# A two-layer hybrid decoder step: three plain fp32 products rewritten as sums of rounded high and low parts

## The chip, the cores and the metric

The kernel runs on one core of a Trainium2 chip. The metric is the time of one execution in microseconds (us); a smaller number is better. Each time given for a kernel is the median of several executions, and one further execution is profiled instruction by instruction.

## The reference

One inference step goes through two layers. A prompt of 512 tokens and eight single sample tokens are handled together, so that T = 520 columns run through the shared weights. Three places of the layer matter here.

- **Page compression.** The compressed branch of the sparse attention cuts the cached key and value rows into blocks of 32 tokens at a stride of 16 and passes each through a small two-layer network: `gelu(flat @ w1) @ w2`, where `flat` has 32 x 64 numbers per block. Keys and values have weights of their own. There are 32 cached pages of 128 rows, four for each of the eight samples, and the prompt's own rows are compressed in the same way.
- **Channel mean.** The convolution branch normalizes its 256 channels: `mu = mean(x)`, `xc = x - mu`, and so on.
- **Pointwise product.** After that normalization and a swish follows `y @ w_pw + b_pw` with a 256 x 256 matrix.

## The kernel before, in words

The kernel keeps channels on the 128 partitions and tokens along the columns. Each big projection (24 tiles of `w_in`, 8 tiles of `w_out` per layer) is made by `product` (L744): both operands were split beforehand into a high part, rounded to the type float32r (`F32R`), and a low part, the rest, and three products high x high, high x low and low x high are added in PSUM. A split (`split`, L724) is two instructions: a copy that rounds, and a subtraction that gives the rest. One tile of a projection takes 8 chunks x 3 products x 2 halves of 260 columns (`HALF`, L362) = 48 matmuls.

Three products still run on plain fp32 operands:

- `compress` (L878) is called four times in a layer, for keys and values (`kv`) and for two groups of pages (`hb`). It multiplies eight 128 x 128 chunks of `w1` (loaded in `cmp_weights`, L867) by the pages, ten at a time: 160 moving columns, or 112 for the last seven pages of the first group. That is 16 matmuls for a call, 64 for a layer.
- `conv_norm` (L1070) makes the channel mean with the constant matrix `mean_w` (L1078, four matmuls of 260 columns for a layer).
- `conv_norm` makes the pointwise product with `raw`, the weights `w_pw` (L1100, eight matmuls of 260 columns for a layer).

Nothing is issued where it stands in the code. The functions only record operations (`Plan.add`, L236), grouped into units; a unit is one operation, or several of the tensor engine under `plan.burst()`. `Plan.place` (L286) then puts the units into the sequence of a long list of numbers, `order` (L395), and gives each buffer the first fitting place when its turn comes. Within an engine the instructions run in that sequence; engines wait for one another by semaphores. Where an elementwise operation may run on one of several engines (`ch(...)`), the letter string `engines` (L386) says which: v is VectorE, s ScalarE, g GpSimd. All loads and stores go out on SyncE's queue; a page of the cache needs its number read from the page table first (`paged`, L611, with the register load at L616). All recorded operations are issued from one line, L352, so that the profile shows that line for nearly everything, and instructions are told apart by engine, operation and shape.

Buffers live in regions (L383): the region `d` has five places of 2,560 columns, and each page tile `pg` takes one of them, as do `x4`, `yo`, `zc` and `yoh`.

Of the kernel before, what the change touches and what calls it, by code (L numbers as in the profile page):

```python
# [9 lines left out]
F32R = mybir.dt.float32r  # L10
# [179 lines left out]
class Plan:  # L190
# [135 lines left out]
    def emit(self, tc, ctx):  # L326
# [60 lines left out]
        "vvvvgvvsssssvssgsvvggvggsvsvvssvvsgvvssvsvggsvvvgvgssgsggvvvgvsgsgsgvvggvvvsvvvvvssvsvsvsgggsvvvsvsgvgvsvgvgvssv"  # L387
        "vvsgsgsvssgvvsggsvgvsgsvsvggsvsggsvvggvggggvvssgvsssvsvsvggvvsgsgvggvvgvvgsssssggggssssvssssssvgvvggvvsvsvsgsgvv"
        "vsvvsvgsvvgvggssvvssvsvvvsvgvggggsgsvvgggggsvgvgvsssgvssvsssssvssssvsssgggvvvggsvgvvvvgvgsssssvvssvvsvvsgvvggsgg"
        "ggvggvvgvgsvvvvgsgsvvvsvgvsvsgvgsgsvsvsvsvggsvsgssggssvsvvvgvvgvgvggsvvsssvsvsssvssvgvvsssggggggvgvvvgsgsvvgssvg"  # L390
        "vsvgvsvvgsvssggvvsvgvvgvvggvsvvvvsvgvgvssvggsvvvsvssvgvsgvggvgsvggsgsgsgvgggvsggggvvvssgsvsvvsvsvsgggsgggvggvggs"
        "gsggssggssssvgsssvsvssvsgggsgvvsggvggvggvsggvssvsgvsgggssssvssvsvvvsssgvvggvggsgvvsssgggvgvgvsssssssssvsvvsvvsss"
        "sgvgvgvgvgvgvvvggvssvvvvssgvsvsvvsggvsgggvvsgsggvvsgsvgvsgggsggvsgggsgsgsvsvsvsvggvv"
    ),
    "order": (  # L395
# [146 lines left out]
def step_kernel(ctx: ExitStack, tc: tile.TileContext, i, o, tune=None):  # L542
# [82 lines left out]
    def constants():  # L625
        ve.memset(ones, 1.0)
        sc.activation(junk, ones[:, :1], AF.Exp)
        ve.memset(mean_w, 1.0 / 256.0)
        warm = plan.bank("warm", "t")
        for n in range(WARM // 2):  # L630
            with plan.burst():
# [85 lines left out]
    def layer(l):  # L717
        z_ = Layer()
# [824 lines left out]
```

## Time and profile before

| | us |
|---|---|
| median of 3 runs | 624.89 |
| lowest and highest run | 624.7, 625.42 |
| profiled execution, its own time | 623.73 |
| profiled execution, span from first to last instruction | 622.0 |
| TensorE matmul (PE) busy | 606.4 |
| TensorE weight load (PEld) busy | 536.7 |
| VectorE (DVE) busy | 433.7 |
| ScalarE (ACT) busy | 259.7 |
| GpSimd (POOL) busy | 226.2 |

A matmul's record lasts longer than the time until the next one can start, since matmuls are pipelined. The time that a matmul takes from its neighbours is therefore read as the distance from start to start (the pitch), and a row of a stretch of equal matmuls gives it as (length of the stretch - length of one record) / (count - 1). A plain fp32 matmul shows as two records, a matmul on float32r operands as one.

### The profile page before, as it was taken

To read this page: it belongs to the slowest core of one execution; us is meant where nothing else is said; L and a number is where in the kernel's file an instruction comes from. 1 tells how busy PE (TensorE), PEld (TensorE's weight loads), DVE (VectorE), ACT (ScalarE), POOL (GpSimd) and SP (SyncE) were. 2 spreads that over 40 slices of the span, in tenths; PEclk is the share of its full clock that TensorE was granted. 3 is DMA by queue.
4 is the path that set the end of the run, shared out by engine and by line. 5 is a ranking of instruction groups with operands and counts; after the bars stand their busy time and mean duration, and the time that the engine had idled before them with its cause. 6 is when DMAs were issued, how large, how long until landed. Compare 5 with 4: busy or idle time off the path is not lost.

```text
span 622.0 us, 15002 instructions
## 1 busy us (share of the span) xinstructions
PE 606.4 (97%) x5526; PEld 536.7 (86%) x5526; DVE 433.7 (70%) x1222; ACT 259.7 (42%) x731; POOL 226.2 (36%) x250
## 2 busy tenths in 40 slices
PE   6999999999999999999999999999999999999997
PEld 5999998898868788579999999999985968677997
DVE  6535879966778697965465498887677678688221
ACT  4102125656683395431221132237575769543100
POOL 2123225442414363341522242556443535144700
PEclk9999999999999999999999999999999999999999
DMA  8755444322652346887546234342246135788622
GB/s 267 217 166 180 152 124 146 115 76 73 136 122 65 104 125 220 268 252 228 185 143 194 85 113 160 94 124 62 77 79 155 37 95 140 185 255 252 208 77 95
DMA packets 89130, 90.98 MB, mean 146 GB/s; under 512 B 25858, under 2 KB 59746, under 8 KB 88930
## 3 DMA queue, kind: packets, MB, share of 16 engines
q1 hardware_dynamic: 89058, 90.04, 48.9%
q8 instruction: 43, 0.70, 0.5%
q14 instruction: 29, 0.24, 0.1%
HBM read 75.32 MB, written 14.67 MB: 145 GB/s over the span
## 4 chain that ended last, share of the span: by engine, by line
PE 84%; DVE 6%; SPq 5%; DMA 3%; issue 2%; ACT 1%; ACTq 0%; DVEq 0%
PE banks L352 84%; DVE t L352 4%; SPq L352 3%; DVE small L352 2%; DMA t<-in_win 2%; SPq L616 1%; ACT t L352 1%; DMA t<-in_x 1%; DMA t<-in_cmp 0%; DVE keep L352 0%; ACTq L352 0%; DVEq L352 0%
## 5 line engine op out<-in xcount | busy, mean ns | idle before, releaser
L352 PE MATMUL banks<-t,t 128*128 128x260 f32 (+5 forms) x3960 | 490.0, 302 | 1.9 <-DVE t L352 0.8
L352 PEld LDWEIGHTS banks<-t,t 128*128 128x128 f32 (+3 forms) x3960 | 434.2, 178 | 32.8 <-issue 25.1
L352 POOL TENSOR_TENSOR t<-t,t 128x512 fp32r<-128x512 f32 (+4 forms) x84 | 111.4, 1332 | 129.2 <-PE banks L352 55.7
L352 ACT ACTIVATE t<-t 128x512 fp32r<-128x512 f32 (+4 forms) x130 | 78.5, 613 | 155.1 <-DVE t L352 56.8
L352 ACT ACTIVATE t<-t,small 128x384 f32<-128x384 f32 (+4 forms) x185 | 99.2, 552 | 16.2 <-DVE small L352 15.9
L352 PE MATMUL banks<-keep,t 128*128 128x128 f32 (+7 forms) x698 | 87.2, 311 | 1.9 <-DVE t L352 1.1
L352 DVE TENSOR_TENSOR t<-t,t 128x512 fp32r<-128x512 f32 (+3 forms) x92 | 71.0, 782 | 22.0 <-PE banks L352 16.0
L352 PEld LDWEIGHTS banks<-keep,t 128*128 128x128 f32 (+2 forms) x698 | 66.5, 161 | 22.1 <-issue 12.5
L352 DVE TENSOR_TENSOR t<-banks,t 128x520 f32<-128x520 f32 (+1 forms) x54 | 37.2, 693 | 63.8 <-PE banks L352 51.2
L352 DVE CUSTOM_DVE_ANT_0 t<-banks,keep,small 128x384 f32<-128x384 f32 (+3 forms) x128 | 64.3, 528 | 16.2 <-PE banks L352 16.0
L352 POOL TENSOR_SCALAR t<-t 128x512 fp32r<-128x512 f32 (+2 forms) x49 | 34.6, 707 | 88.3 <-PE banks L352 48.5
L352 ACT ACTIVATE t<-banks 128x512 f32<-128x512 f32 (+3 forms) x72 | 36.6, 525 | 62.1 <-PE banks L352 45.7
L352 PE MATMUL banks<-t,keep 128*32 128x130 f32 (+7 forms) x688 | 41.2, 306 | 6.7 <-DVE keep L352 4.8
L352 PEld LDWEIGHTS banks<-t,keep 128*32 128x32 f32 (+3 forms) x688 | 23.2, 116 | 20.5 <-DVE keep L352 5.0
L352 POOL TENSOR_SCALAR t<-t,small 128x384 f32<-128x384 f32 (+3 forms) x50 | 32.9, 671 | 21.2 <-DVE small L352 15.4
L352 ACT ACTIVATE small<-small 128x32 f32<-128x32 f32 (+3 forms) x76 | 23.5, 310 | 27.5 <-DVE small L352 27.4
L352 DVE COPY t<-banks 128x512 f32<-128x512 f32 (+2 forms) x37 | 21.5, 589 | 11.2 <-PE banks L352 7.3
L352 DVE SCALAR_TENSOR_TENSOR t<-t,t 128x520 f32<-128x520 f32 (+2 forms) x32 | 27.8, 873 | 1.3 <-ACT t L352 1.1
L352 POOL TENSOR_TENSOR t<-t,keep 128x520 f32<-128x520 f32 (+1 forms) x11 | 14.2, 1296 | 33.5 <-DVE t L352 20.4
L352 POOL TENSOR_TENSOR t<-t 128x520 f32<-128x520 f32 (+1 forms) x12 | 12.8, 1068 | 33.2 <-DVE t L352 13.9
L352 ACT ACTIVATION_READ_ACCUMULATOR t<-t,small 128x1 f32 x132 | 24.7, 187 | 0.0
L352 DVE SCALAR_TENSOR_TENSOR small<-small 128x130 f32<-128x130 f32 (+3 forms) x80 | 23.5, 296 | 1.5
(81 smaller groups left out, 358.1 us busy)
## 6 DMA issues: line engine op xcount, KB each, us to landing
t<-in_w_in SPq DMA_DIRECT2D x96, 256.0 KB
t<-in_cmp SPq DMA_DIRECT2D x64, 128.0 KB
t<-in_slc SPq DMA_DIRECT2D x64, 128.0 KB
t<-in_w_out SPq DMA_DIRECT2D x32, 256.0 KB
t<-in_x SPq DMA_DIRECT2D x16, 260.0 KB
t<-in_win SPq DMA_DIRECT2D x16, 256.0 KB
out_win<-t SPq DMA_DIRECT2D x16, 256.0 KB
t<-glu SPq DMA_DIRECT2D x12, 264.0 KB
```

What stands on the lines that cost most here:

```text
L352: fn(*[real(v) for v in o.a], **{k: real(v) for k, v in o.k.items()})
L616: pages[n] = tc.nc.sync.value_load(pt.real(plan)[0:1, n:n + 1], min_val=0, max_val=n_phys - 1)
```

## The change

The weights `w1` are split once a layer, into two more buffers each (`cmp_weights`). In `compress` each half of a page group is split into a high and a low part, both in one new buffer of the kind `pg`, and each plain matmul becomes three on float32r parts, in one burst. In `conv_norm` the input of the mean is split and multiplied, high and low, by a rounded copy of the constant matrix (1/256 is exact in it): two matmuls for one. The pointwise weights and its input are split, and three matmuls take the place of one. The string `engines` has 816 letters where it had 756 (60 more choices, 30 splits of two), and both lists are new from end to end.

```diff
+    mean_r = new("c", [128, 128], F32R, fixed=True)
...
         ve.memset(mean_w, 1.0 / 256.0)
+        ve.tensor_copy(mean_r, mean_w)
...
         def cmp_weights():
...
-                z_.w1.append(w)
+                parts = [new("w1", [128, 8, 128], F32R) for u in "hl"]
+                split(w, *parts, "gv")
+                z_.w1.append(parts)
...
         def compress(kv, pg, first):
...
-            w, nb = z_.w1[kv], 17 if first else 20
+            (wh, wl), nb = z_.w1[kv], 17 if first else 20
...
             for h, (a, b) in enumerate(((0, 10), (10, nb))):
-                xs = pg[h][:, :b - a].rearrange("p b (k c g q) -> p k c g b q", k=2, c=8, g=2)[:, kv]
+                src = pg[h][:, :b - a, 128 * kv:128 * kv + 128]
+                parts = new("pg", [128, 2, 10, 128], F32R)
+                parts = [parts[:, u, :b - a] for u in range(2)]
+                split(src, *parts)
+                xh, xl = (v.rearrange("p b (c g q) -> p c g b q", c=8, g=2) for v in parts)
                 for cc in range(8):
-                    te.matmul(po[:, :, a:b], w[:, cc, :], xs[:, cc], start=(h == cc == 0), stop=(cc == 7),
-                              skip_group_check=True)
+                    with plan.burst():
+                        for n, (w, x_) in enumerate(((wh, xh), (wh, xl), (wl, xh))):
+                            te.matmul(po[:, :, a:b], w[:, cc, :], x_[:, cc], start=(h == cc == n == 0),
+                                      stop=(cc == 7 and n == 2), skip_group_check=True)
...
         def conv_norm():
...
+            wh, wl = (new("wpw", [128, 2, 256], F32R) for u in "hl")
+            split(raw, wh, wl, "gv")
...
             for c in range(2):
+                parts = [P("cy", F32R) for u in "hl"]
+                split(yv[c], *parts)
                 with plan.burst():
-                    for k, (a, b) in enumerate(HALF):
-                        te.matmul(pm[:, k], mean_w, yv[c][:, a:b], start=(c == 0), stop=(c == 1))
+                    for n, v in enumerate(parts):
+                        for k, (a, b) in enumerate(HALF):
+                            te.matmul(pm[:, k], mean_r, v[:, a:b], start=(c == n == 0), stop=(c == n == 1))
...
+                parts = [P("cy", F32R) for u in "hl"]
+                split(yv[c], *parts)
+                z_.cy.append(parts)
...
-                for c in range(2):
+                for c, (yh, yl) in enumerate(z_.cy):
                     with plan.burst():
-                        for k, (a, b) in enumerate(HALF):
-                            te.matmul(pm[:, k], raw[:, c, 128 * m:128 * m + 128], yv[c][:, a:b], start=(c == 0), stop=(c == 1))
+                        for n, (w, v) in enumerate(((wh, yh), (wh, yl), (wl, yh))):
+                            for k, (a, b) in enumerate(HALF):
+                                te.matmul(pm[:, k], w[:, c, 128 * m:128 * m + 128], v[:, a:b],
+                                          start=(c == n == 0), stop=(c == 1 and n == 2))
```

## Rows read from the trace of the kernel before

**Rows 1.** The page's head and part 1: busy time, share, instructions.

```profile
span 622.0 us, 15002 instructions
...
PE 606.4 (97%) x5526; PEld 536.7 (86%) x5526; DVE 433.7 (70%) x1222; ACT 259.7 (42%) x731; POOL 226.2 (36%) x250
```

**Rows 2.** The page's part 4: the chain that ended last, by engine.

```profile
PE 84%; DVE 6%; SPq 5%; DMA 3%; issue 2%; ACT 1%; ACTq 0%; DVEq 0%
```

**Rows 3.** Waits of PE: in total us, times, longest us.

```profile
PE banks L352 <- DVE keep L352: 4.8, 1, 4.8
PE banks L352 <- DVE t L352: 2.8, 5, 0.9
PE banks L352 <- POOL t L352: 1.0, 1, 1.0
PE banks L352 <- DMA t<-in_win: 0.8, 2, 0.7
PE banks L352 <- DMA t<-in_cmp_w: 0.6, 1, 0.6
PE banks L352 <- ACT t L352: 0.6, 1, 0.6
PE banks L352 <- DMA t<-in_cmp: 0.5, 1, 0.5
PE banks L352 <- DVE small L352: 0.4, 1, 0.4
```

**Rows 4.** Stretches: length, busy us (instructions) of PE, PEld, DVE, ACT, POOL; PEclk, DMA, GB/s.

```profile
12.00:62.00 50.00, 47.85 (x415) 46.15 (x416) 25.16 (x62) 10.53 (x20) 12.80 (x11) 1.00 0.63 191
311.00:370.00 59.00, 59.00 (x555) 56.52 (x554) 37.79 (x89) 11.23 (x21) 16.59 (x15) 1.00 0.44 138
```

**Rows 5.** Groups of PE by form, whole span: busy us, mean ns of a record.

```profile
L352 PE MATMUL banks<-t,t 128*128 128x260 f32 x3104 | 413.6, 289 | 0.8 <-DVE t L352 0.8
...
L352 PE MATMUL banks<-t,t 128*128 128x160 f32 x192 | 36.2, 303 | 1.1 <-DMA t<-in_cmp_w 0.6 <-DMA t<-in_cmp 0.5
...
L352 PE MATMUL banks<-t,t 128*128 128x112 f32 x64 | 10.3, 271 | 0.0
...
L352 PE MATMUL banks<-t,keep 128*128 128x260 f32 x16 | 3.9, 389 | 0.0
```

**Rows 6.** PE in order of time, four stretches: start us, length us, first form, count.

```profile
57.50 2.06 PE L352 MATMUL banks<-t,t 128*128 128x160 f32 x14
...
197.95 1.92 PE L352 MATMUL banks<-t,keep 128*128 128x260 f32 x8
...
230.60 0.82 PE L352 MATMUL banks<-t,t 128*128 128x260 f32 x3
...
280.76 13.97 PE L352 MATMUL banks<-t,t 128*128 128x260 f32 x115
```

**Rows 7.** Narrow plain matmuls: a group in 48.9 to 49.35, two timeline rows.

```profile
L352 PE MATMUL banks<-t,t 128*128 128x112 f32 x4 | 0.6, 271 | 0.0
...
250.62 0.36 PE L352 MATMUL banks<-small,keep 128*128 128x6 f32 x2 [0.40 <-DVE small L352]
250.84 0.37 PE L352 MATMUL banks<-t,t 128*128 128x260 f32 x1
```

**Rows 8.** Instructions of today's splits, by form, one row for each engine and operation.

```profile
L352 DVE CAST t<-t 128x512 fp32r<-128x512 f32 x27 | 12.4, 464 | 4.0 <-DMA t<-in_w_in 3.6 <-PE banks L352 0.3
...
L352 DVE TENSOR_TENSOR t<-t,t 128x512 fp32r<-128x512 f32 x76 | 60.6, 804 | 21.8 <-PE banks L352 16.0 <-POOL t L352 3.1 <-issue 1.2
...
L352 ACT ACTIVATE t<-t 128x512 fp32r<-128x512 f32 x72 | 44.9, 627 | 80.6 <-DMA t<-in_w_in 22.0 <-DMA t<-in_w_out 17.4 <-POOL t L352 12.8
...
L352 POOL TENSOR_TENSOR t<-t,t 128x512 fp32r<-128x512 f32 x68 | 91.9, 1355 | 116.0 <-PE banks L352 55.3 <-ACT t L352 33.2 <-DVE t L352 16.5
```

**Rows 9.** Chain of waits between 21 and 50 us, shares.

```profile
by line: SPq L352 44.4%; SPq L616 27.3%; issue 20.9%; DMA t<-in_cmp 7.7%
```

More of the change, by code (lines that the diff above doesn't have):

```diff
@@ L386 @@
     "engines": (
[L387 to L393, printed above, removed]
+        "gssvssgssvvsssvsggvvsgvvvvgvsvsvsvsvsgvvvvvvsssvsssssssvsvsvvvvsssssgsggvvgvgvvvsvgvsvsgvvvsgvvsvsgsvvggvvssvvvv"
+        "sgvvsgssggvsvvgsvssvvvsgsvvvssvvgsggsvgvsvvggvggsgsgsgvgsgvvvsvggsggssssvsgvggggvsvggsgsgvsssvsvgsvvsvvsgsvvvsss"
+        "vsvvgsgvgvvvgvggvggvvsvvsssvvsvsvsvssssvvssvsssggvvsgggggggsvssgvgvgvgssgsgvssgggssvssvssvssssvsssssssvggvvsggvg"
+        "vggggvgssssvsvgsvvssssgsgsgvvggggsvgvvvvsvggsgsvvgggsgsgggvvvvsvvvsvgvgvvsgggvgsvvssvsgsvgvvvvvvggvvgvvgsvsvssvs"
+        "gsvvvvvssggssvsvvvggvggvvssvgvsgsvvvsvgvsvsvvvsvvggsvvvgvvvsvsggsvgsvvvgsvvgsvvvgvvsvgggvssvvgsgsgsvsgvgvgggsvsv"
+        "vvsgsvvvsgsggvssvsvsgssgvgsssvsvsvgvgsgsvsgggvggvvssggsvsgvggssssvssvssvvvvggsgvgsgggggvsvggsggggsvsvvvvgvvssvss"
+        "sssvsvvggvvsgvgsvggvggsgvvggsggvssvsgggssggvsgsssvsvsvsssssvsggsvvvgvsgvgvvggsssvssvvgsvvsvssggvgsgsgsgggsgggvgv"
+        "vvsvsggvsggvgvgvgggvgvgvsgvvsggv"
     ),
     "order": (
[140 rows of a table removed]
[143 rows of a table added]
     ),
@@ L1071, in conv_norm @@
             yv = z_.conv
+            z_.cy = []
             raw = new("wpw", [128, 2, 256])
             ld(raw, i["w_pw"][l])
+            wh, wl = (new("wpw", [128, 2, 256], F32R) for u in "hl")
+            split(raw, wh, wl, "gv")
             pm = plan.bank("pm", "mm", 2)[:, :, :T // 2]
             for c in range(2):
+                parts = [P("cy", F32R) for u in "hl"]
+                split(yv[c], *parts)
                 with plan.burst():
-                    for k, (a, b) in enumerate(HALF):
-                        te.matmul(pm[:, k], mean_w, yv[c][:, a:b], start=(c == 0), stop=(c == 1))
+                    for n, v in enumerate(parts):
+                        for k, (a, b) in enumerate(HALF):
+                            te.matmul(pm[:, k], mean_r, v[:, a:b], start=(c == n == 0), stop=(c == n == 1))
             sq = []
```

283 rows, old and new, of the table TUNE are left out of this document.

## The prediction

> **What bounds the kernel now.** I read the busy times first. The tensor engine has a record open for 606.4 of 622.0 us, every other engine has 188 us or more to spare [rows 1]. The chain that ended last agrees: 84% of it is PE [rows 2]. Then I asked who keeps PE waiting: the eight waits sum to 11.5 us, of which 4.8 us is the single wait at the very start [rows 3]. So some 7 us of the whole run is PE standing still for somebody, and whatever adds work to PE adds it to the end. The reader should see that elsewhere a microsecond is nearly free, and on PE it costs a microsecond. The two stretches that hold the page compression, one in each layer, say the same: PE is busy for 47.85 of 50 us in the first and for all 59 us of the second, while VectorE, ScalarE and GpSimd are free for half the time or more in the first, and VectorE for a third in the second [rows 4].
>
> So the change must be costed in PE's pitch, start to start. Four stretches give it. A record of the plain compression at 160 columns: (2.06 - 0.303) / 13 = 0.135 us [rows 5, 6], two records, so **0.270 us** a matmul. A plain record at 260 columns: (1.92 - 0.389) / 7 = 0.219 us for the mean, (0.82 - 0.389) / 2 = 0.22 for the pointwise product [rows 5, 6], **0.438 us** a matmul. A float32r matmul at 260 columns in the projections: (13.97 - 0.289) / 114 = **0.120 us** [rows 5, 6].
>
> Two of these show something else. If a plain record sweeps its columns twice, one sweep of 260 costs 0.219 / 2 = 0.110 us, and the float32r matmul at 0.120 is slower than its one sweep: the columns are not what paces it. And narrow plain records do not get cheaper in proportion: at 160 columns 0.135, at 112 columns (0.6 - 0.271) / 3 = 0.11 rather than the 0.095 of the proportion, and at 6 columns still (250.84 - 250.62) / 2 = 0.11 [rows 7]. Each record has a weight load of its own, 5526 for 5526 [rows 1]. I read this as a floor: a load of 128 fp32 weight columns paces the engine at 0.110 to 0.120 us, however few columns follow.
>
> **The change, part by part.**
>
> *Compression.* Today 192 records x 0.135 + 64 x 0.11 = 25.9 + 7.0 = 32.9 us. After it, 128 matmuls become 384, each one record. None has more than 160 columns, so each is under the floor. No row shows a float32r matmul with fewer than 260 columns and 128 weight columns, so I bound it: from below by the plain floor of 0.110 (384 x 0.110 = 42.2 us), from above by the wider float32r matmul, 0.120 (46.1 us). Same operand type as the upper, fewer columns: I take 0.116, 44.5 us. That is **+11.6 us** (+9.3 to +13.2). The change triples the number of weight loads and saves only sweeps, and at this width the sweeps were the smaller part.
>
> The Trainium skill's page "TensorE: Matmul & The Clock Gate" says under "Back-to-back issue gap" that a warm matmul costs N / 2.4 + 2.5 ns, which is 69 and 49 ns at 160 and 112 columns and 111 at 260; by that alone compression would cost 24.6 us, mean and pointwise 1.7 us less each, and the run would take about 613 us. The same page under "LDWEIGHTS" puts a load at columns / 1.2, 107 ns for 128, which is the floor; the rows with 6 columns side with this one.
>
> *Mean.* 16 records x 0.219 = 3.5 us become 16 matmuls x 0.120 = 1.9: **-1.6 us**. *Pointwise.* 32 records x 0.219 = 7.0 us become 48 x 0.120 = 5.8: **-1.2 us**. Both lose sweeps and gain few loads, as at 260 columns they should.
>
> *Splits.* 30 copies and 30 subtractions are new. In columns, per layer: 2,048 for `w1`, 9,472 for the pages, 2,592 in the normalization; over two layers 28,224, or 55 pieces of 512. A piece costs 0.46 to 0.63 us to copy and 0.80 (VectorE) to 1.36 us (GpSimd) to subtract [rows 8], in all some 70 to 110 us, spread over three engines with 946 us to spare [rows 1]. I cost them at nothing, because PE's other work covers them: in the first layer the projections of keys, values and queries, in the second those and no wait at all [rows 4]. If that cover fails in places, it is the second rival. The one copy of the mean matrix at the start (128 columns) stands ahead of nothing but a later product. Loads from memory are the same in number and size.
>
> *Order and engines.* Both lists are new throughout, so each queue is rearranged, SyncE's too. In the first layer the pages arrive one at a time behind SyncE's register loads and issues, which hold the chain from 21 to 50 us [rows 9], and PE fills that time with projections. The new sequence has the same interleaving: compression units among projections in both layers. Bounds: it could take back at most the 6.7 us of waits behind the start [rows 3], and could lose as much. Nearest to nothing: 0.
>
> *Sum.* 11.6 - 1.6 - 1.2 = **+8.8 us** on the profiled execution's 623.73, which is 1.16 under the median of 624.89. On the median: **633.7 us**. By the bounds of the pitch alone the sum is +6.5 (floor 0.110 for all three) to +10.4 (0.120).
>
> **The rivals.**
>
> *A. Narrow matmuls pace by their columns (faster).* If float32r loads hide fully, the pitch is 110 / 260 = 0.42 ns a column and the 10 ns that the wide ones show on top: 78 ns at 160, 57 at 112. Compression then takes 288 x 0.078 + 96 x 0.057 = 27.9 us, -5.0; with mean and pointwise -7.8, **617 us**. It decides where the pitch falls under 0.086 (32.9 / 384). For it: float32r is one sweep and no row shows it narrow. Against it: six plain columns cost 0.11 [rows 7], and 260 float32r columns cost more than a sweep. Chance 0.15.
>
> *B. Splits become PE's wait (slower still).* Each half of a page group needs 2.5 pieces copied, then subtracted, 3.2 to 5 us by [rows 8], before its 24 matmuls (2.8 us). The parts take one of five places of region `d`, four of which the page tiles hold at first, so two halves can't be split at once there. In the first layer the pages also come late [rows 9]. If four of the first layer's eight halves keep PE waiting for 2 us each, that is +8: **641 us**. Against it: PE's queue has projections between. Chance 0.12.
>
> *C. The new order regains what PE loses.* It would need all 6.7 us of waits and 2 us of tighter changes between tile shapes: **625 us**, no change. Against it: behind the start no single wait is longer than 1 us and seven kinds of releaser share them [rows 3], so there is no one place to mend. Chance 0.08, of which 0.03 ends faster.
>
> *D. The narrow parts are not single sweeps.* Then each of the 384 costs what a plain one does, 288 x 0.270 + 96 x 0.22 = 98.9 us, +66: **688 us**. Against it: the projections' 3,072 matmuls have one record each [rows 5], on parts made by the same split. Chance 0.03.
>
> **How the numbers follow.** The forecast (628 to 640) has 0.62. The range 618 to 643 takes in the bounds of the pitch with 6 us either way for the order, B up to 643, and C; it leaves out D and most of A, under 0.2. A measurement of this kernel can tell a change of about 0.2% (1.25 us). Faster: A and a part of C, 0.18. Same: the rest of C, 0.05. Slower: forecast, B and D, 0.77.
>
> **What would show it.** PE's records rise by 144 (304 of the three plain products become 448), to about 5,670. The rows with 160 and 112 columns read 288 and 96 and stand 0.110 to 0.120 us apart; if 0.06 to 0.08, A is right and I am wrong. Rows of 260 columns with 0.219 are gone. PE's share stays at 97%, and PE's waits stay near 11 us; if they double, with compression's splits as releasers between 12 and 65 us, it is B. The forecast is wrong if the time is under 627.

## The result, and the profile after

The changed kernel takes **634.81 us** (median of 4 runs, 633.13 to 636.71); the kernel before took 624.80 beside it (4 runs, 624.41 to 625.42). The ratio is 1.016, with a 95% interval of 1.013 to 1.019: 10 us slower, give or take 2. The forecast was 633.7 with a range of 618 to 643.

To compare kernels that ran on different occasions I use their ratios to the kernel before, measured beside each; 0.1% is 0.62 us.

The profiled execution's head, its busy times (busy us, share, instructions) and the engine shares of the chain that ended last:

```profile
span 633.1 us, 15357 instructions
...
PE 616.6 (97%) x5670; PEld 550.4 (87%) x5670; DVE 470.5 (74%) x1253; ACT 274.3 (43%) x754; POOL 240.0 (38%) x257
...
PE 62%; DVE 6%; DMA 2%; ACT 2%; issue 1%; POOL 0%; SPq 0%; DVEq 0%; POOLq 0%; ACTq 0%
```

This chain is followed back to 167 us only and its shares sum to 73%, so its 62% is not to be set beside the 84% of [rows 2].

Against [rows 1], PE has 144 records and 10.2 us of busy time more, and the span is 11.1 us longer. VectorE has 36.8 us more, ScalarE 14.6 and GpSimd 13.8: that is the work of the splits. PE is still busy for 97% of the span. So the extra time is mostly PE at work, not PE waiting. What it works on is in the groups by form (count, then busy us and mean ns of a record):

```profile
L352 PE MATMUL banks<-t,t 128*128 128x260 f32 x3120 | 408.7, 287 | 5.0 <-DVE t L352 3.2 <-POOL t L352 1.7
L352 PE MATMUL banks<-t,t 128*128 128x160 f32 x288 | 38.8, 274 | 0.0
L352 PE MATMUL banks<-t,t 128*128 128x112 f32 x96 | 13.0, 266 | 0.0
...
L352 PE MATMUL banks<-t,keep 128*128 128x260 f32 x16 | 2.4, 291 | 0.2 <-DVE small L352 0.2
```

The counts are the forecast ones, 288 and 96 in place of the 192 and 64 of [rows 5], so every narrow matmul is one record now. Their pitch is best read from the weight loads, since the matmuls' ends are modelled. The group of loads from 66.46 to 69.2 us, all of them for matmuls of 160 columns (mean length 192 ns):

```profile
L352 PEld LDWEIGHTS banks<-t,t 128*128 128x128 f32 x25 | 2.9, 192 | 0.2 <-issue 0.2
```

The loads in order of time (start us, length us, count), eleven for matmuls of 112 columns and then these 25:

```profile
44.84 1.30 PEld L352 LDWEIGHTS banks<-t,t 128*128 128x128 f32 x11
...
66.45 2.87 PEld L352 LDWEIGHTS banks<-t,t 128*128 128x128 f32 x25 [0.20 <-issue]
```

The pitch is (1.30 - 0.192) / 10 = 0.111 at 112 columns and (2.87 - 0.192) / 24 = **0.1116 us** at 160. 384 of the latter are 42.9 us, against the 32.9 worked out for the plain compression. The last view is who keeps PE waiting (us in total, times, longest us):

```profile
PE banks L352 <- DVE t L352: 4.9, 8, 1.4
PE banks L352 <- ACT t L352: 1.8, 2, 1.3
PE banks L352 <- DVE keep L352: 1.8, 2, 1.1
PE banks L352 <- POOL t L352: 1.7, 3, 0.8
PE banks L352 <- ACT keep L352: 0.4, 1, 0.4
PE banks L352 <- DVE small L352: 0.2, 1, 0.2
```

They sum to 10.8 us, against 11.5 in [rows 3]. Those of the first 14 us:

```profile
PE banks L352 <- DVE t L352: 1.9, 2, 1.4
PE banks L352 <- ACT t L352: 1.3, 1, 1.3
PE banks L352 <- DVE keep L352: 1.1, 1, 1.1
```

Four waits of 4.3 us together have taken the place of the single one of 4.8 us at the start, and the waits behind it sum to 6.5 us, against 6.7 before. The start differs in another way too. The stretch from 8 to 15 us (busy and count of PE, PEld, VectorE, ScalarE, GpSimd; PEclk, DMA share, GB/s), first in the kernel before, then in the changed one:

```profile
8.00:15.00 7.00, 7.00 (x85) 5.49 (x84) 6.15 (x10) 4.39 (x8) 4.08 (x3) 1.00 0.94 333
```

```profile
8.00:15.00 7.00, 5.50 (x34) 4.57 (x35) 6.57 (x9) 4.27 (x7) 3.45 (x3) 0.51 1.01 363
```

Behind waits of 1.3 us before a burst at 6.53 and 1.4 us before one at 8.97, PE was granted half of full speed there, 1.2 GHz rather than 2.4. The kernel of section 1 with all three products plain, in the same sequence, reads 0.57 in this stretch, so the loss belongs to the sequence and not to the rounding. It is not in every execution: the profiled one of the kernel with the compression alone rounded reads 1.00. As an estimate from these rows, 7 us at half speed cost at most 3.5 us.

### The profile page after: what moved, and what is told of

Its sections match the earlier page's. It is cut to its first block, busy times and chain, and to the rows that moved or that the text cites. A ratio compares the mean times of both kernels' runs of the same rounds, so it can differ in the third digit from the quotient of the medians.

```text
span 633.1 us, 15357 instructions
## 1 busy us (share of the span) xinstructions
PE 616.6 (97%) x5670; PEld 550.4 (87%) x5670; DVE 470.5 (74%) x1253; ACT 274.3 (43%) x754; POOL 240.0 (38%) x257
## 4 chain that ended last, share of the span: by engine, by line
PE 62%; DVE 6%; DMA 2%; ACT 2%; issue 1%; POOL 0%; SPq 0%; DVEq 0%; POOLq 0%; ACTq 0%
PE banks L352 62%; DVE t L352 5%; DVE small L352 2%; ACT t L352 1%; DMA t<-in_w_in 1%; DMA cv<-t 0%; POOL t L352 0%; SPq L352 0%; ACT small L352 0%; ACT keep L352 0%; DVEq L352 0%; DVE keep L352 0%; POOLq L352 0%; ACTq L352 0%
## 5 line engine op out<-in xcount | busy, mean ns | idle before, releaser
L352 PE MATMUL banks<-t,t 128*128 128x260 f32 (+4 forms) x4104 | 495.2, 297 | 5.0 <-DVE t L352 3.2
L352 POOL TENSOR_TENSOR t<-t,t 128x512 fp32r<-128x512 f32 (+5 forms) x92 | 126.4, 1382 | 138.6 <-PE banks L352 42.8
L352 ACT ACTIVATE t<-t 128x512 fp32r<-128x512 f32 (+6 forms) x141 | 91.3, 658 | 163.3 <-DVE t L352 56.2
L352 DVE TENSOR_TENSOR t<-t,t 128x512 fp32r<-128x512 f32 (+8 forms) x114 | 100.8, 897 | 15.2 <-POOL t L352 5.8
L352 POOL TENSOR_SCALAR t<-t 128x512 fp32r<-128x512 f32 (+5 forms) x63 | 48.9, 780 | 118.6 <-PE banks L352 48.6
L352 PE MATMUL banks<-keep,t 128*128 128x128 f32 (+8 forms) x698 | 85.4, 311 | 1.0 <-DVE t L352 0.8
L352 PEld LDWEIGHTS banks<-keep,t 128*128 128x128 f32 (+3 forms) x698 | 66.0, 161 | 19.4 <-issue 8.2
L352 DVE CUSTOM_DVE_ANT_0 t<-banks,keep,small 128x384 f32<-128x384 f32 (+3 forms) x128 | 64.3, 529 | 14.3 <-PE banks L352 13.7
L352 DVE CAST t<-t 128x512 fp32r<-128x512 f32 (+5 forms) x45 | 26.6, 594 | 4.6 <-DMA t<-in_w_in 1.8
L352 ACT ACTIVATE small<-small 128x32 f32<-128x32 f32 (+2 forms) x79 | 24.4, 309 | 10.4 <-DVE small L352 10.3
L352 DVE TENSOR_TENSOR small<-small 128x130 f32<-128x130 f32 (+6 forms) x66 | 23.3, 355 | 0.8
```

The costliest lines, as they stand in the source:

```text
L352: fn(*[real(v) for v in o.a], **{k: real(v) for k, v in o.k.items()})
```

## The experiments

**The theory** at the outset: compression pays 0.111 us for each of its 384 matmuls because each carries a load of 128 weight columns, and a microsecond on PE is a microsecond at the end. **Its rivals**: the new sequence costs the time, the splits hold PE up, or the columns set the pace. All experiments but one start from the changed kernel and keep its sequence and its engine letters for every operation that is left; the exception says so.

### 1. Which part of the change costs the time

Four kernels ran together. The first takes all three products back to plain fp32:

```diff
-                parts = new("pg", [128, 2, 10, 128], F32R)
...
-                split(src, *parts)
...
-                        for n, (w, x_) in enumerate(((wh, xh), (wh, xl), (wl, xh))):
...
+                    te.matmul(po[:, :, a:b], w[:, cc, :], xs[:, cc], ...)
...
-                split(yv[c], *parts)
...
+                        te.matmul(pm[:, k], mean_w, yv[c][:, a:b], start=(c == 0), stop=(c == 1))
```

> The changed kernel's sequence and engine choice, with all three products plain fp32 again and no split of theirs. Theory (the time is the tensor engine's pitch; the sequence is nearly neutral): the rounding adds 9.8 (compression at 0.111 us a load) less 2.8 us (mean and pointwise), so 634.8 - 7.0 = 628, and between 625 and 628 if a part of the 3 us that the sum lacks is the sequence's. Rival 1 (the new sequence is what costs): 632 or more. Rival 2 (the splits keep PE waiting): 625 or less.

Measured: 626.04 us, ratio 1.0013 (0.999 to 1.0035). The sequence by itself adds 0.8 us, and 0 to within its interval.

The second takes back the mean and the pointwise product alone:

```diff
         def conv_norm():
...
-            split(raw, wh, wl, "gv")
...
-                split(yv[c], *parts)
...
```

> The changed kernel with mean and pointwise product plain again, the compression rounded. Theory: 2.8 us above the changed kernel, 637 to 638, since 28 more column sweeps of 260 come back and nothing else. Rival 1 (sequence): within 1 us of 634.8. Rival 2 (splits in the normalization are waits on the way to the end): 634 or less.

Measured: 635.65 us, 1.0166 (1.013 to 1.0202). Against the first this is +1.53%, or 9.6 us, for the compression alone.

The third takes back the compression alone:

```diff
         def cmp_weights():
...
-                split(w, *parts, "gv")
-                z_.w1.append(parts)
+                z_.w1.append(w)
...
         def compress(kv, pg, first):
...
-                split(src, *parts)
...
```

> The changed kernel with the compression plain again, mean and pointwise rounded. Theory: 634.8 - 9.8 = 625 us, and 2.8 us under the kernel with all three plain in this sequence. Rival 1 (sequence): 632 or more. Rival 2 (splits): the compression's splits go with it, so the saving is larger than the 9.8 us of PE's pitch, 622 or less.

Measured: 625.67 us, 1.0009 (0.9985 to 1.0033). The changed kernel lies 1.51%, or 9.4 us, above it. So the compression costs 9.4 to 9.6 us by two pairs, each with some 2.5 us of uncertainty. The mean and the pointwise product, rounded, give back 0.2 us here (1.0009 against 1.0013) and 0.4 us there (1.016 against 1.0166), with the same uncertainty. The forecast was 2.8.

What they gain and a part of what they lose can be seen, since PE's work stands in the same sequence in both kernels. The mean of the first layer (start us, length us), first in the kernel with all products plain, then in the one with those two rounded:

```profile
197.40 1.92 PE L352 MATMUL banks<-t,keep 128*128 128x260 f32 x8
```

```profile
198.38 1.20 PE L352 MATMUL banks<-t,keep 128*128 128x260 f32 x8
```

That is 0.7 us for a layer. In the second layer the same 50 projection matmuls, again first in the one and then in the other (PE's idle time and its releaser in brackets):

```profile
519.69 7.17 PE L352 MATMUL banks<-t,t 128*128 128x260 f32 x50
```

```profile
515.04 4.55 PE L352 MATMUL banks<-t,t 128*128 128x260 f32 x36
520.23 0.73 PE L352 MATMUL banks<-t,t 128*128 128x260 f32 x4 [0.64 <-DVE t L352]
521.75 2.38 PE L352 MATMUL banks<-t,t 128*128 128x260 f32 x10 [0.79 <-POOL t L352]
```

PE reaches them 4.7 us earlier, but they end only 2.7 us earlier. VectorE and GpSimd haven't come forward as far: PE waits for the split of this projection's weights, which VectorE's copy ends at 520.17 us and GpSimd's subtraction at 521.70. At 530.68 us follows a wait of 0.5 us for ScalarE. The other pair shows the same: these 50 take 7.17 us with the two products plain and 8.88 in the changed kernel, with waits of 0.43 and 0.78.

The two profiled spans, 624.7 and 622.4, differ by 2.3 us in the forecast's direction. One execution each against a median that hardly moved doesn't settle what the two products are worth. It stays open between 0 and 2.8.

The fourth keeps all splits but leaves out both cross products of the compression:

```diff
-                        for n, (w, x_) in enumerate(((wh, xh), (wh, xl), (wl, xh))):
+                        for n, (w, x_) in enumerate(((wh, xh),)):
```

> The changed kernel with one matmul of each three in the compression (high x high); the products with the low parts are left out, all splits stay. 256 matmuls fewer. Theory (PE's pitch goes straight to the end, the splits are covered): 256 x 0.111 = 28.4 us less, 606 us. Rival 2 (splits keep PE waiting): PE would stand where the matmuls were, a saving of less than 20 us, 615 or more.

Measured: 626.18 us, 1.002 (0.9995 to 1.0046). **This missed.** 256 matmuls fewer at 0.1116 us are 28.6 us, and 1.4%, or 8.7 us (give or take 2.5), came back. Its busy times, and the first two rows of PE's waits:

```profile
PE 595.6 (95%) x5414; PEld 526.9 (84%) x5414; DVE 469.4 (75%) x1253; ACT 274.0 (44%) x754; POOL 242.6 (39%) x257
```

```profile
PE banks L352 <- DVE t L352: 13.6, 11, 4.2
PE banks L352 <- DVE small L352: 2.4, 4, 1.9
```

PE lost 21.0 us of busy time, not 28.6, and its waits on VectorE grew from 4.9 to 13.6 us; all its waits sum to 23.4 us, against 10.8. The longest of them is 4.25 us in the second layer. SyncE, VectorE and PE around it, in order of time (start us, length us):

```profile
327.80 0.36 SPq L352 DMA_DIRECT2D t<-rs  x1
```

```profile
335.67 0.70 DVE L352 TENSOR_TENSOR t<-banks,t 128x520 f32<-128x520 f32 x1 [6.89 <-DMA t<-rs]
```

```profile
336.43 0.80 PE L352 MATMUL banks<-t,t 128*128 128x260 f32 x3 [4.25 <-DVE t L352]
```

The normalization's row `rs` goes through memory to be spread over the partitions. VectorE can apply it only 7.9 us after the DMA was issued, and the next projections need it. Those spreads of this run whose landing the trace tells land some 3 us after their issue, so this one is late; two page loads were issued just ahead of it, but what held it up was not followed. In the changed kernel the same spread is issued at 335.30 us and PE has no wait between 320 and 345 us: compression's matmuls run meanwhile. The granted clock fell too. PE's stretch from 60 to 80 us (busy and count of PE, PEld, VectorE, ScalarE, GpSimd; PEclk, DMA share, GB/s), first in the changed kernel, then in this one:

```profile
60.00:80.00 20.00, 20.00 (x185) 18.97 (x185) 15.36 (x42) 6.74 (x13) 3.20 (x4) 1.00 0.44 149
```

```profile
60.00:80.00 20.00, 17.56 (x136) 15.63 (x133) 17.10 (x46) 6.75 (x14) 4.39 (x5) 0.83 0.46 150
```

Where PE stood still for 1.92 us before a burst at 57.09 and for 2.04 us before one at 64.61, the stretch behind was granted 0.83 of full speed on average instead of 1.00, that is, a part of it at 1.2 GHz rather than 2.4. So some of what was left ran slower.

The theory needed a second sentence after this: **adding to PE and taking away from PE are not the same price**. The next runs test that, and the pace itself.

### 2. Load or columns, adding, splits alone, and wider matmuls

Fewer columns, 62% of them, and as many weight loads; left out are the cross products of all but four pages of each half:

```diff
                         for n, (w, x_) in enumerate(((wh, xh), (wh, xl), (wl, xh))):
-                            te.matmul(po[:, :, a:b], w[:, cc, :], x_[:, cc], ...)
+                            e = b if n == 0 else a + 4
+                            te.matmul(po[:, :, a:e], w[:, cc, :], x_[:, cc, :, :e - a], ...)
```

> The changed kernel, but the two cross products of the compression run over the first 4 pages of each half alone (64 columns of 160 or 112); the high times high product keeps all. Left out: the cross products of the other pages. As many matmuls and weight loads, 256 of them with about half the columns or fewer. Theory (pace of the weight load): the 64-column matmuls also follow one another at 0.11 us and the time stays within 1.5 us of the changed kernel's 634.8. Rival (pace of the columns): 64 columns pass in about 0.05 us, 256 x 0.06 = 15 us less TensorE time, and the end comes 5 to 15 us earlier, 620 to 630.

Measured: ratio 1.0186 (1.0155 to 1.0217), 637.64 us beside 626.93 for the kernel before. No gain at all over 1.016. The same stretch as above, loads and matmuls from 66.46 to 69.2 us by form, and then the loads in order of time:

```profile
L352 PEld LDWEIGHTS banks<-t,t 128*128 128x128 f32 x26 | 3.0, 192 | 0.2 <-issue 0.2
...
L352 PE MATMUL banks<-t,t 128*128 128x160 f32 x9 | 2.9, 325 | 0.0
L352 PE MATMUL banks<-t,t 128*128 128x64 f32 x16 | 2.7, 254 | 0.0
```

```profile
66.39 2.98 PEld L352 LDWEIGHTS banks<-t,t 128*128 128x128 f32 x26 [0.20 <-issue]
```

(2.98 - 0.192) / 25 = 0.1115 us: two of three matmuls have 64 columns instead of 160, and the loads follow one another as before. The columns don't set the pace; something that each matmul pays does. That it is the load of 128 weight columns is the reading that fits, since each matmul has one, but no run changed the load's width or let two matmuls share one.

A fourth product, low times low, in every chunk:

```diff
-                        for n, (w, x_) in enumerate(((wh, xh), (wh, xl), (wl, xh))):
+                        for n, (w, x_) in enumerate(((wh, xh), (wh, xl), (wl, xh), (wl, xl))):
```

> The changed kernel with a fourth product, low times low, in every chunk of the compression: 128 more narrow rounded matmuls, nothing else. Theory (what is added on TensorE here goes to the end one for one): 128 x 0.111 = 14.2 us, 648 to 650. Rival (TensorE has slack in these stretches, which the compression fills while it waits for pages, norms and splits): a part of the 14.2 us disappears in waits, under 643.

Measured: 649.35 us, 1.0368 (1.0342 to 1.0393). That is 2.1%, or 13.0 us (give or take 2.5), over the changed kernel, of the 14.3 that 128 x 0.1116 makes. Its busy times:

```profile
PE 631.8 (98%) x5798; PEld 565.2 (87%) x5798; DVE 466.2 (72%) x1253; ACT 273.8 (42%) x754; POOL 241.2 (37%) x257
```

PE's busy time grew by 15.2 us over the changed kernel's. What is added on PE does go to the end, nearly one for one.

All the splits, but one plain product of the high parts in place of three rounded ones; the low parts are computed and left unused:

```diff
-                        for n, (w, x_) in enumerate(((wh, xh), (wh, xl), (wl, xh))):
-                            te.matmul(po[:, :, a:b], w[:, cc, :], x_[:, cc], ...)
+                        te.matmul(po[:, :, a:b], r32(wh[:, cc, :]), r32(xh[:, cc]), ...)
```

> The changed kernel with all its splits of weights and pages, but the compression takes one plain fp32 matmul of the high parts per chunk in place of three rounded products (the low parts are computed and not used). Theory (the splits cost nothing, the whole price is the third matmul's worth of TensorE time): as the kernel with plain compression, 624.5 to 627. Rival (the splits hold TensorE up, and the rounded products only show it): 630 to 635.

Measured: 627.44 us, 1.0009 (0.9987 to 1.0031), the very ratio of the kernel with plain compression and no splits (1.0009). Its busy times show that the splits are there:

```profile
PE 608.6 (97%) x5542; PEld 540.6 (86%) x5542; DVE 469.5 (75%) x1253; ACT 274.0 (44%) x754; POOL 242.0 (39%) x257
```

VectorE is as busy as in the changed kernel (470.5), PE is 8.0 us less so. As long as PE has 33 us of compression to do, the splits are hidden, to within some 2 us. The price is the matmuls'.

Wider matmuls: half as many loads over the same columns. Both halves of a page group are split, 64 columns at a time, into one tile, and one matmul covers 20 or 17 pages. It is the one kernel whose sequence is not just the changed kernel's, thinned out: its splits, and the page loads that wait for a place in the region `d`, stand elsewhere in it.

```diff
-            for h, (a, b) in enumerate(((0, 10), (10, nb))):
...
-                for cc in range(8):
+            for j in range(2):
+                parts = new("pg", [128, 2, 20, 64], F32R)
+                for h, (a, b) in enumerate(((0, 10), (10, nb))):
...
+                    split(src, parts[:, 0, a:b], parts[:, 1, a:b])
...
+                for cc in range(4):
...
+                            te.matmul(po, w[:, 4 * j + cc, :], x_[:, cc], ...)
```

> The same rounded products over the same columns in half as many matmuls: the two halves of a batch half's pages are split 64 columns at a time into one tile, so that one matmul runs over 20 pages (320 columns) or 17 (272) in place of two over 160 and 160 or 112. 192 matmuls instead of 384. Theory (a narrow rounded matmul costs its weight load, 0.111 us): 192 at 0.12 to 0.14 us, so 23 to 27 us of TensorE instead of 42.6, 16 to 20 us fewer; if all of it came back at the end the time would be 615 to 619, if only the share that came back when two of three products were left out (8.6 of 28.4 us), 629 to 630. Rival (they cost their columns, 0.8 ns each): pitch 0.22 to 0.26, time as the changed kernel, 634 to 636. Second rival (the splits of both halves must now be done before the first matmul): more idle TensorE ahead of the bursts, time 636 to 640.

Measured: 663.52 us, 1.0581 (1.055 to 1.0612), **slower by 26 us** than the changed kernel. The matmuls did what was expected of them, near enough. The loads of twelve matmuls of 272 columns, then of nine of 320:

```profile
44.49 1.75 PEld L352 LDWEIGHTS banks<-t,t 128*128 128x128 f32 x12
...
407.44 1.54 PEld L352 LDWEIGHTS banks<-t,t 128*128 128x128 f32 x9
```

With a length of 0.193 for a load these are (1.75 - 0.193) / 11 = 0.142 and (1.54 - 0.193) / 8 = 0.168 us. At these widths the columns show in the pace, and 96 of each make 30 us where 384 narrow ones made 42.9. But the pages came late. SyncE's loads of pages in the changed kernel, between 40 and 70 us, and then in this one:

```profile
40.02 4.77 SPq L352 DMA_DIRECT2D t<-in_cmp  x5
50.16 1.46 SPq L352 DMA_DIRECT2D t<-in_cmp  x2
54.34 6.18 SPq L352 DMA_DIRECT2D t<-in_cmp  x6
66.77 0.34 SPq L352 DMA_DIRECT2D t<-in_cmp  x1
```

```profile
51.92 10.38 SPq L352 DMA_DIRECT2D t<-in_cmp  x10
64.97 5.94 SPq L352 DMA_DIRECT2D t<-in_cmp  x6
```

By the kernel's code the tiles of split parts hold places of region `d` that the next pages need; the trace shows the late loads, not which tile held them up. SyncE's queue runs in order, so the spread of `rs` goes out behind those loads, at 62.40 us instead of 51.80. VectorE waits 12.3 us for it and applies it at 66.36 us; after that it splits the late pages, until 79.4 us. PE stands behind both (idle time and its releaser in brackets):

```profile
71.05 0.66 PE L352 MATMUL banks<-t,keep 128*32 128x130 f32 x8 [6.72 <-DVE small L352]
80.30 1.17 PE L352 MATMUL banks<-t,t 128*128 128x320 f32 x3 [8.59 <-DVE small L352]
```

That is 15.3 us in two waits, the longest of 40.7 us that PE waits in all, against 10.8 in the changed kernel. This run answers the pace, not whether a wider form with a good sequence would win: that wasn't tried.

### 3. What keeps the removed time from coming back

Two more kernels ran together. The first is the one with high x high alone, and now without the subtractions too (the low parts of weights and pages are not computed, 20 instructions fewer):

```diff
-                split(w, *parts, "gv")
+                ch("svg").copy(parts[0], w)
...
-                split(src, *parts)
+                ch("svg").copy(parts[0], src)
```

> The kernel with one rounded product per chunk (626.2 us, 28.4 us of TensorE's work fewer than the changed kernel), and now also without the second step of every split of the compression: the low parts of weights and pages are not computed, 20 subtractions fewer on VectorE and GpSimd. Theory (with the products gone, TensorE there waits for pages from the DMA queue and for the norm's spread, which the splits only follow): within 2 us of 626.2. Rival (the splits end last): the waits of 2.0 and 2.1 us on VectorE at 62 and 374 us and what stands like them go, 621 to 623.

Measured: 621.61 us beside 627.68 for the kernel before, 0.9901 (0.9873 to 0.9928). That is 1.2%, or 7.4 us (give or take 2.3), faster than with the subtractions (1.002): **my theory missed, the rival holds**. Its busy times, and the first row of PE's waits:

```profile
PE 596.3 (96%) x5414; PEld 527.0 (85%) x5414; DVE 444.5 (72%) x1236; ACT 274.3 (44%) x754; POOL 232.0 (37%) x254
```

```profile
PE banks L352 <- DVE t L352: 10.0, 11, 3.0
```

PE is as busy as with the subtractions, VectorE has 25 us less to do. PE's waits on VectorE fall from 13.6 to 10.0 us and those on its small tiles from 2.4 to 0.2; those on ScalarE rise from 2.3 to 4.0, and all of them together fall from 23.4 to 19.9. The two profiled spans differ by 3.3 us only, so the size lies between 3.3 and 7.4. The splits do stand in PE's way, but only once the matmuls that covered them are gone.

The second takes the kernel with plain compression, which has no splits there, and leaves out 4 of the 8 chunks of every compression:

```diff
-                for cc in range(8):
+                for cc in range(4):
```

> The kernel with plain compression and rounded mean and pointwise product (625.7 us), with 4 of the 8 chunks left out of every compression: 64 plain matmuls fewer, 16.4 us of TensorE's time, no splits in it. Theory (what is taken off TensorE in these stretches comes back only in part, since pages and the norm chain end last there): 620 to 624. Rival (only the splits held the earlier kernel up, TensorE is the bound): all of it comes back, 609 to 611.

Measured: 622.49 us, 0.9929 (0.9904 to 0.9955). Of 16.4 us taken off PE, 0.8%, or 5.0 us (give or take 2.2), came back, here without any split of the compression in the way. The spread of `rs` is one place again. What VectorE and PE wait for there, from 320 to 340 us:

```profile
DVE t L352 <- DMA t<-rs: 6.2, 1, 6.2
```

```profile
PE banks L352 <- DVE t L352: 3.6, 1, 3.6
```

Over the whole run PE's busy time is 12.0 us less than with all eight chunks and its waits sum to 20.1 us, against 11.2. The wait of 3.6 us is the longest of them; the others were not followed one by one. So compression's matmuls are a cover for two things at least: the splits, and the normalization's way through memory.

The kernel without subtractions is faster than the changed kernel, and by 1.0% faster than the kernel before. It computes less, though: its compression is one product of rounded operands and keeps no low parts, so it is no replacement for either. No kernel of this study that keeps the cross products was faster than the kernel before.

## Why the prediction was right, and where it was not

- **The bound.** "whatever adds work to PE adds it to the end" held: +14.3 us of matmuls gave +13.0. Its other half, that "elsewhere a microsecond is nearly free, and on PE it costs a microsecond", is not true backwards: 28.6 us fewer gave 8.7, and 16.4 fewer gave 5.0, about three tenths. The stretches of [rows 4], with PE busy throughout, could not show that. They show that PE is covered, not what would end last if it were not.
- **Compression, +11.6 forecast.** The mechanism held as far as it was tested (a pace per matmul that the columns don't set), and the term was over-sized. The pitch is 0.1116, not the 0.116 I chose between 0.110 and 0.120, which makes +10.0 by PE's count; the paired runs give 9.4 to 9.6. The value lay near the lower bound: the rows with 6 columns [rows 7] were nearer to it than the projections' 0.120, whose 260 columns cost a little of their own.
- **Mean and pointwise, -2.8 forecast.** Their matmuls did what was worked out (16 records of 0.389 us are now 16 of 0.291, and the plain pointwise records are gone), but the runs show 0.2 to 0.4 us with an uncertainty of 2.5. This step, "Both lose sweeps and gain few loads", counted PE's time and took it for the end's, which is the half of the bound that failed: in the second layer PE comes earlier and waits some 2 us between 519 and 531 us for VectorE, GpSimd and ScalarE, where it doesn't wait with the two products plain. Whether that is the whole of it was not tested.
- **Splits, 0 forecast.** Shown: 1.0009 with and without them, each give or take 0.0024. Their work was estimated at 70 to 110 us, and the three engines are 65 us busier. The cover I named (projections) was not all of it: without the cross products the subtractions cost 3.3 to 7.4 us, so compression's own matmuls are cover too.
- **Order, 0 forecast.** Measured +0.8 (-0.6 to +2.2). The waits behind the start did not move (6.7 to 6.5 us); the granted clock of 0.51 between 8 and 15 us is a place where the new sequence loses.
- **The sum.** 9.5 + 0.8 - 0.3 = 10.0, against 10.0 measured and +8.8 forecast. These parts are differences between ratios that lead from one kernel to the other, so they must add up and prove nothing more. Two terms of the forecast were off by about 2 in opposite directions; that the total came within 1.2 us is in part luck. One bound was added up wrongly: with 0.110 for all three products the sum is +5.8, not +6.5, which leaves mean and pointwise at 0.120.
- **The rivals.** A (pace by columns, 617) is out: the pitch is 0.111 to 0.1116 at 160 and 112 columns, and still with two in three cut to 64. The Trainium skill's page "TensorE: Matmul & The Clock Gate" gives N / 2.4 + 2.5 ns for an isolated matmul under "Back-to-back issue gap" and says itself that this counts too little at small N, where loads take their share; as an estimate it makes 29 ns at 64 columns, and the loads 111.5 ns apart say otherwise. Its section "LDWEIGHTS" gives columns / 1.2, which for 128 is 107 ns, and there the trace agrees within 5 ns. B (splits as PE's wait, 641) is out for this kernel, and true for the one with a third of the matmuls. C (order regains it) and D (not single sweeps) are out by the runs of section 1 and by the counts.

## What to carry to other kernels

Count weight loads, not only sweeps: a rounded product of three matmuls for one pays where a plain record takes more than 1.5 times the load's 0.1116 us (two records against three), that is, at 260 columns (0.219) and not at 160 (0.135) or 112 (0.11). That is PE's time only: at 260 columns the medians here don't show the gain. A busy engine on the path is a price for what is added to it, not for what is taken away: before counting a saving, look for what its work covers, here a 7.9 us trip through memory and a row of splits. To see a cover, remove the covering work; in the profile in which that work is there, no wait tells of it.

## What the runs showed of the hardware that was not expected

Rounded matmuls with 128 weight columns follow one another at 0.111 to 0.1116 us at 112 and 160 columns and with two in three cut to 64; at 0.120 for 260 [rows 6], 0.142 for 272 and 0.168 for 320. The step between 260 and 272 columns, 22 ns, is larger than the 12 columns account for at the slope of the wider ones, (0.168 - 0.142) / 48 = 0.54 ns a column, or 6.5 ns; why was not tried. And a PE that is given less to do can be granted less clock: 0.83 from 60 to 80 us in the kernel with a third of the products, 1.00 there in the kernel with all of them. The changed kernel has such a stretch too, 0.51 from 8 to 15 us, where its new sequence keeps PE waiting.
